# A PEER decoder trunk on one core: the dense output product takes 224 tokens, the last 32 are gathered by index and added on VectorE

## The chip, the core and the metric

The kernel runs on one core of a Trainium2 chip. The metric is the device time of one execution in microseconds. The kernel before took a median of 1882.46 us in three runs (1881.70, 1882.46 and 1882.48).

## The reference, cut to what matters

Two layers, 256 tokens of 1024 columns. Each layer has a trunk (three groups of mixing heads and an output projection) and then a PEER block. In the PEER block every token chooses, for each of 8 heads, 16 of 128 x 128 = 16,384 single-neuron experts, so 128 experts in all, each with a gate:

```python
experts = e1 * N_KEYS + e2                      # (tokens, 128 choices)
gates = softmax(sv)                             # of the 16 best scores per head
hid = gelu(einsum("td,tkd->tk", xi, u_tab[ei])) # one hidden value per token and choice
out = einsum("tk,tkd->td", gates * hid, v_tab[ei])
x = x + out
```

## The kernel before, in words

The kernel doesn't gather. It computes the hidden values of all 16,384 experts for all 256 tokens, multiplies them by a dense matrix of gates that is zero except at the chosen experts, and multiplies the result by the whole table `v`. An expert is a pair (a, j): a lies on the 128 partitions, j runs over 128 steps. All products are made of two float32r parts, hi and lo: hi x hi, lo x hi and hi x lo.

`trunk` makes queries, keys, values, the convolution and the recurrence, and the output projection; `add_rows` (L187 to L209) adds a result of a product to the residual `x` and scales its rows; `norm_tail` (L224) transposes the normed rows into `XH` and `XL` for the next stage. `peer` (L597) has these stages:

- queries and scores, then top-16 searches and decoding on VectorE, which lie beside the first 18 pairs of the hidden product (`J1=36`). `turn` (L737) transposes chosen indices and gates of 128 tokens into `eH`, `eT`, `gT`.
- the hidden product (`hpair`, L811): for a pair j, j+1, 2 x 24 matmuls of 256 columns (L172 to L174) with the blocks of `u` as weights and the normed activations as moving operand. ScalarE applies the GELU into `ab3[:, j, token]`.
- `quad` (L768): for four tokens, 8 matmuls of 128 columns (L798) build the dense gates from one-hot rows that VectorE (L776, L782, L792) and ScalarE (L789) make; the result is multiplied into `ab3` or put where a later `hpair` multiplies it. 64 quads for 256 tokens, spread over the 46 pairs after the first 18.
- the output product (`out_step` L841, `accumulate` L239): for each j the block `v[l, :, j, :]` (128 x 1024, 512 KB, queue SP, L151) is split into hi (ScalarE, L163) and lo (VectorE, L164), the coefficients `ab3[:, j, :]` of 256 tokens into `chl` (ScalarE L846, VectorE L847). The coefficients are the weights of the matmul, `v` is the moving operand: per j two token halves x two column halves x three products, 12 matmuls of 512 columns into four PSUM banks (L250, L251, L252). The last `TAIL=2` steps go bank by bank, so that the first token half is ready before the second.

Three buffers each for `raw`, `hi` and `lo`, two for `chl` (tag `hg`). The order of the instructions on each engine is fixed when the program is built, by a scheduler that follows the order of the source and priorities; `load` and `split` have a high priority, so they run ahead as far as buffers allow.

Of the kernel before, what the change touches and what calls it, by code (L numbers as in the profile page):

```python
# [35 lines left out]
CW = 661  # L36
# [9 lines left out]
def hymba_peer_kernel(  # L46
# [28 lines left out]
    WARM=12,  # L75
):
# [4 lines left out]
    dr_p = ctx.enter_context(tc.tile_pool(name="dr", bufs=1, space=bass.MemoryType.DRAM))  # L81
    xd = [dr_p.tile([P, D], F32, name=f"xd{i}") for i in range(2)]
# [20 lines left out]
    ab3 = ab.rearrange("p (n t) -> p n t", t=T)  # L103

# [36 lines left out]
    # products of zeros: the tensor engine's clock is up when the first rows arrive  # L141
# [11 lines left out]

    def split(r, w=D, after=None):
        hi = spl_p.tile([P, w], F32R, tag="hi", name="hi")
        lo = spl_p.tile([P, w], F32R, tag="lo", name="lo")
        with ExitStack() as es:
            if after:
                for ins in after:
                    es.enter_context(tc.issue_after(ins.ins))  # L160
            else:
                es.enter_context(tc.high_priority(offset=0))
            S.activation(out=hi, in_=r, func=AF.Copy)  # L163
            V.tensor_tensor(out=lo, in0=r, in1=hi.bitcast(F32), op=ALU.subtract)  # L164
# [21 lines left out]
    def add_rows(tt, ps, gb):  # L186
        # the residual, its rows' scales, and its product with the gains  # L187
# [76 lines left out]

    def log1p_exp_neg_abs(dst, z, n, tag):
# [3 lines left out]
        # exp(-|z|) = ((1 - t) / (1 + t)) ** 4 with t = tanh(|z| / 8)  # L269
# [8 lines left out]
        # log1p(e) = 2 atanh(e / (2 + e))  # L278
# [10 lines left out]
    def trunk(l, mx_p, prev, gb):  # L289
# [44 lines left out]
        # values and forget gates, in the layout [token, column]  # L334
# [41 lines left out]
        # log(1 + exp(-|z|)) of the forget gates and of the recurrence's lambda  # L376
# [9 lines left out]
        # cumulative log forget gates as rank-two terms of the logits  # L386
# [29 lines left out]
        # conformer convolution  # L416
# [19 lines left out]
        def layer_norm():  # L436
# [16 lines left out]
            # a Newton step: y (1.5 - 0.5 v y^2)  # L453
# [10 lines left out]
        # gated linear recurrence  # L464
# [30 lines left out]
        def rnn_scan():  # L495
            # -expm1(2 log_a) = tanh(-log_a) (1 + a^2)
# [10 lines left out]
            # sqrt(v) = v y (1.5 - 0.5 v y^2)  # L507
# [11 lines left out]
        # attention  # L519
# [61 lines left out]
        # output projection and residual  # L581
# [13 lines left out]
    def peer(l, oh_p, wq, next_gain):  # L595
# [108 lines left out]
        def decode_index(tt, s):  # L704
            # sum over ranks a of (a == chosen rank) * index[a]
# [31 lines left out]
        def turn(tt):  # L737
            b = bankb()
            for s in range(3):
                TE.transpose(b[:, s * P:(s + 1) * P], ea[:, tt, s, :], ident)  # L740
            sl = slice(tt * P, (tt + 1) * P)
            S.activation(out=eH[:, :, sl], in_=b[:, 0:2 * P].rearrange("p (s t) -> p s t", t=P),
                         func=AF.Copy)
            S.activation(out=eT[:, sl], in_=b[:, P:2 * P], func=AF.Copy)
            # the scaled gate as two float16 parts, each kept as float32
            g = b[:, 2 * P:3 * P]
            gh = sm_p.tile([P, P], F16, name="gh", bufs=1)
# [243 lines left out]
```

## Time and profile before

| | |
|---|---|
| median of the runs shown | 1882.46 us (1881.70 to 1882.48) |
| span of the profiled execution, first to last instruction | 1879.8 us |
| own time of the profiled execution | recorded by its span alone; the runs lie 1.9 to 2.7 us above it |
| TensorE (PE) busy | 1850.7 us, 98% |
| VectorE (DVE), ScalarE (ACT), GpSimd (POOL) busy | 1358.5, 1196.0, 28.1 us |
| TensorE's granted clock | 0.998 of 2.4 GHz over the span |
| moved by DMA | 328.86 MB, mean 175 GB/s |

How to read it: PE is one engine with a fixed order; "busy" counts overlapping matmuls once, and a matmul's own duration is longer than the distance to the next start, because they are pipelined. The rate of a stream is therefore taken from start to start. PEld is the weight load that goes with every matmul. An idle entry names what ended the wait.

### The profile page before, as it was taken

To read this page: it belongs to the slowest core of one execution; us is meant where nothing else is said; L and a number is where in the kernel's file an instruction comes from. 1 tells how busy PE (TensorE), PEld (TensorE's weight loads), DVE (VectorE), ACT (ScalarE), POOL (GpSimd) and SP (SyncE) were. 2 spreads that over 40 slices of the span, in tenths; PEclk is the share of its full clock that TensorE was granted. 3 is DMA by queue.
4 is the path that set the end of the run, shared out by engine and by line. 5 is a ranking of instruction groups with operands and counts; after the bars stand their busy time and mean duration, and the time that the engine had idled before them with its cause. 6 is when DMAs were issued, how large, how long until landed. Compare 5 with 4: busy or idle time off the path is not lost.

```text
span 1879.8 us, 33413 instructions
## 1 busy us (share of the span) xinstructions
PE 1850.7 (98%) x12688; PEld 1672.3 (89%) x12688; DVE 1358.5 (72%) x2902; ACT 1196.0 (64%) x2345; POOL 28.1 (1%) x34
## 2 busy tenths in 40 slices
PE   9999999999999999999999999999999999999998
PEld 8889999999998888888897899999999988888886
DVE  6969987778885555555688699777788755555555
ACT  5954668888874444444469455598888744444444
POOL 0100000000000000000010000000000000000000
PEclk9999999999999999999999999999999999999999
DMA  6264555555555655555543545655555565555554
GB/s 228 91 210 154 168 184 168 160 167 166 163 166 202 211 188 186 188 190 188 184 156 118 174 152 172 193 160 166 168 159 169 167 213 191 186 187 189 190 190 136
DMA packets 90016, 328.86 MB, mean 175 GB/s; under 512 B 9984, under 2 KB 9984, under 8 KB 89600
## 3 DMA queue, kind: packets, MB, share of 16 engines
q1 hardware_dynamic: 88704, 322.54, 52.8%
q10 hardware_dynamic: 1152, 4.19, 0.6%
q8 instruction: 99, 1.62, 0.3%
q14 instruction: 61, 0.50, 0.1%
HBM read 323.55 MB, written 3.15 MB: 174 GB/s over the span
## 4 chain that ended last, share of the span: by engine, by line
PE 89%; DVE 8%; ACT 2%; issue 1%; POOL 0%; DMA 0%; POOLq 0%; SPq 0%; ACTq 0%
PE bank L172 14%; PE bank L174 14%; PE bank L173 14%; PE bankb L251 13%; PE bankb L250 13%; PE bankb L252 13%; PE bankb L798 3%; DVE lo L164 3%; PE bank L651 1%; DVE ab L627 1%; DVE ab L625 1%; DVE ab L626 1%; DVE ab L624 1%; PE bank L231 0%; DVE ab L623 0%
## 5 line engine op out<-in xcount | busy, mean ns | idle before, releaser
L164 DVE TENSOR_TENSOR lo<-raw,hi 128x1024 fp32r<-128x1024 f32 (+1 forms) x600 | 734.1, 1225 | 255.6 <-ACT hi L163 252.1
L163 ACT ACTIVATE hi<-raw 128x1024 fp32r<-128x1024 f32 (+1 forms) x600 | 630.5, 1053 | 262.8 <-PE bank L173 126.3
L172 PE MATMUL bank<-XH,hi 128*128 128x256 f32 x2560 | 732.0, 286 | 0.0
L174 PE MATMUL bank<-XH,lo 128*128 128x256 f32 x2560 | 723.0, 282 | 6.2 <-DVE lo L164 6.2
L173 PE MATMUL bank<-XL,hi 128*128 128x256 f32 x2560 | 719.5, 281 | 0.7 <-DVE XL L236 0.7
L174 PEld LDWEIGHTS bank<-XH,lo 128*128 128x128 f32 x2560 | 483.0, 189 | 8.4 <-DVE lo L164 8.2
L172 PEld LDWEIGHTS bank<-XH,hi 128*128 128x128 f32 x2560 | 484.4, 189 | 1.4 <-issue 0.4
L173 PEld LDWEIGHTS bank<-XL,hi 128*128 128x128 f32 x2560 | 483.5, 189 | 1.1 <-DVE XL L236 1.1
L250 PE MATMUL bankb<-hi,chl 128*128 128x512 f32 x1024 | 406.1, 397 | 1.0 <-ACT chl L846 1.0
L251 PE MATMUL bankb<-lo,chl 128*128 128x512 f32 x1024 | 405.5, 396 | 0.0
L252 PE MATMUL bankb<-hi,chl 128*128 128x512 f32 x1024 | 405.3, 396 | 0.0
L846 ACT ACTIVATE chl<-ab 128x256 fp32r<-128x256 f32 x256 | 106.7, 418 | 361.7 <-PE bankb L252 361.7
L789 ACT ACTIVATE ob<-oe,gT 128x128 f16<-128x128 f16 x768 | 251.9, 407 | 0.9 <-DVE oe L782 0.9
L250 PEld LDWEIGHTS bankb<-hi,chl 128*128 128x128 f32 x1024 | 192.7, 188 | 48.7 <-ACT chl L846 2.4
L252 PEld LDWEIGHTS bankb<-hi,chl 128*128 128x128 f32 x1024 | 192.1, 188 | 47.3 <-DVE chl L847 0.7
L251 PEld LDWEIGHTS bankb<-lo,chl 128*128 128x128 f32 x1024 | 192.6, 188 | 45.4
L847 DVE SCALAR_TENSOR_TENSOR chl<-ab,chl 128x256 fp32r<-128x256 f32 x256 | 108.9, 426 | 157.9 <-ACT chl L846 157.9
L776 DVE TENSOR_TENSOR oa<-iota,eH 128x512 f16<-128x512 f16 x128 | 54.2, 424 | 50.1 <-PE bankb L798 49.3
L798 PE MATMUL bankb<-ob,oa 128*128 128x128 f16 x1024 | 74.0, 222 | 0.0
L792 DVE TENSOR_SCALAR ob<-iota_h,eT,gT 128x128 f16<-128x128 f16 x256 | 70.6, 310 | 0.0
L782 DVE TENSOR_TENSOR oe<-iota,eH 128x512 f16<-128x512 f16 x128 | 53.9, 424 | 20.6 <-ACT ob L789 19.7
L798 PEld LDWEIGHTS <-oa 128*128 128x128 f16 x1024 | 60.2, 115 | 4.0
(198 smaller groups left out, 1171.4 us busy)
## 6 DMA issues: line engine op xcount, KB each, us to landing
raw<-in_u_dram SPq DMA_DIRECT2D x256, 512.0 KB, 3.5
raw<-in_v_dram SPq DMA_DIRECT2D x256, 512.0 KB, 4.2
raw<-in_ws_dram SPq DMA_DIRECT2D x32, 512.0 KB, 3.6
raw<-in_wq_dram SPq DMA_DIRECT2D x32, 512.0 KB, 4.0
raw<-in_wo_dram SPq DMA_DIRECT2D x16, 512.0 KB, 3.8
raw<-in_wv_dram SPq DMA_DIRECT2D x8, 528.0 KB, 3.7
ab<-in_g_dram SPq DMA_DIRECT2D x4, 512.0 KB, 5.8
ab<-in_kt_dram SPq DMA_DIRECT2D x2, 1024.0 KB, 6.7
```

The costliest lines, as they stand in the source:

```text
L163: S.activation(out=hi, in_=r, func=AF.Copy)
L164: V.tensor_tensor(out=lo, in0=r, in1=hi.bitcast(F32), op=ALU.subtract)
L172: TE.matmul(out=ps, lhsT=hi[:, k, :], rhs=XH[:, k, :], start=(k == 0), stop=False)
L173: TE.matmul(out=ps, lhsT=hi[:, k, :], rhs=XL[:, k, :], start=False, stop=False)
L174: TE.matmul(out=ps, lhsT=lo[:, k, :], rhs=XH[:, k, :], start=False, stop=(k == KT - 1))
L250: TE.matmul(out=po, lhsT=mh, rhs=hi[:, d0:d0 + 512], start=(m == 0), stop=False)
L251: TE.matmul(out=po, lhsT=mh, rhs=lo[:, d0:d0 + 512], start=False, stop=False)
L252: TE.matmul(out=po, lhsT=ml, rhs=hi[:, d0:d0 + 512], start=False, stop=(m == n - 1))
L789: S.activation(out=ob[:, s, i, :], in_=oe[:, :, i], func=AF.Copy, scale=gT[:, s, t:t + 1])
L798: TE.matmul(out=b[:, i * P:(i + 1) * P], lhsT=oa[:, :, i], rhs=ob[:, s, i, :], start=(s == 0), stop=(s == 1))
L846: S.activation(out=chl[:, 0, :], in_=c, func=AF.Copy, scale=1.0 / GS)
L847: V.scalar_tensor_tensor(out=chl[:, 1, :], in0=c, scalar=1.0 / GS, in1=chl[:, 0, :].bitcast(F32), op0=ALU.mult, op1=ALU.subtract)
```

## The change

`TG=32` tokens leave the dense path, `TD=224` stay in it.

- The output product is turned (`accumulate_turned`): the blocks of `v` are the weights, 8 blocks of 128 columns, and `chl` is the moving operand. Per j and block one matmul of 448 columns (hi x both parts of `chl`, side by side) and one of 224 (lo x the hi part), 16 matmuls into 8 PSUM banks `ot`. `chl` has two tags now, so four buffers, and is written before the load of its step.
- At the layer's end `finish(d)` adds the two halves of a bank (ScalarE copy, VectorE add) and transposes the block back to rows of tokens (two transposes per block).
- The 32 tokens' hidden values are stored to DRAM, 16 values of j at a time (8 stores per layer on ACT's queue, 128 x 16 x 32 numbers). Then 32 indirect DMAs on POOL's queue read back 128 numbers each (`gathered_hidden`: choice i of every token and head group, onto 128 partitions), 32 more gather 128 rows of `v` each, 512 KB (`gathered_sum`), and 32 operations on VectorE multiply a gathered block by its coefficient and add it up in `aG`. They stand beside the steps j = 28 to 119 of the output product. One matmul of 512 columns per column half with a 0/1 matrix then folds the 128 partitions into 32 token rows.
- 56 quads per layer instead of 64.

```diff
+TG = 32
+TD = T - TG
+NG = P // TG
...
+def accumulate_turned(ot, steps, tail, finish):
+        def block(m, st, d):
+            chl, (hi, lo) = st
+            w = slice(d * P, (d + 1) * P)
+            TE.matmul(out=ot[d][:, 0:2 * TD], lhsT=hi[:, w],
+                      rhs=chl.rearrange("p s t -> p (s t)"), start=(m == 0), stop=False)
+            TE.matmul(out=ot[d][:, 0:TD], lhsT=lo[:, w], rhs=chl[:, 0, :], start=False,
+                      stop=(m == n - 1))
...
+        for d in range(KT):
+            for i, st in enumerate(last):
+                block(n - tail + i, st, d)
+            finish(d)
...
+        def gathered_index():
+            V.scalar_tensor_tensor(out=e, in0=e, scalar=float(P), in1=ea[:, 1, 1, :],
+                                   op0=ALU.mult, op1=ALU.add)
...
+            for g in range(NG):
+                for s in range(2):
+                    TE.matmul(out=b[g * TG:(g + 1) * TG, s * TG:(s + 1) * TG],
+                              lhsT=ident[:, P - TG:P],
+                              rhs=ea[:, 1, 2 * s, g * TG:(g + 1) * TG], start=True, stop=True)
...
+        def gathered_hidden():
+            for i in range(TG):
+                G.indirect_dma_start(out=cG[:, i:i + 1], out_offset=None, in_=hd[l],
+                                     in_offset=bass.IndirectOffsetOnAxis(ap=pos[:, i:i + 1], axis=0))
...
+        def gathered_sum(i):
+            r = carve((3, 4, 6)[i % 3] * D, D)
+            G.indirect_dma_start(out=r, out_offset=None, in_=vr_in,
+                                 in_offset=bass.IndirectOffsetOnAxis(ap=idx[:, i:i + 1], axis=0))
...
+            with tc.issue_after(last_lo[0].ins):
...
+                    V.scalar_tensor_tensor(out=aG, in0=r, scalar=c, in1=aG, op0=ALU.mult,
+                                           op1=ALU.add)
...
+            if j % HSTORE == 0:
+                nc.scalar.dma_start(out=hdv[:, j - HSTORE:j, :], in_=ab3[:, j - HSTORE:j, TD:T])
...
-                chl = oh_p.tile([P, 2, T], F32R, tag="hg", name="chl")
-                w = split(load(v_in[l, :, j, :]))
-                c = ab3[:, j, :]
+                chl = oh_p.tile([P, 2, TD], F32R, tag=("hg", "ob")[j // 2 % 2], name="chl")
+                c = ab3[:, j, 0:TD]
...
-            while tq[0] < T // 4 and tq[0] < (jp + 1) * (T // 4) / (rest - QLEAD):
+            while tq[0] < TD // 4 and tq[0] < (jp + 1) * (TD // 4) / (rest - QLEAD):
...
-        pr = [bankb() for _ in range(4)]
+        gathered_hidden()
+        ot = [bankb() for _ in range(4)] + [bank() for _ in range(4)]
...
+        for i in range(TG):
+            j = GHEAD + i * (P - GTAIL - GHEAD) // TG
+            steps[j] = with_sum(i, steps[j])
...
+        def finish(d):
+            tb = carve(9 * D + (d % 2) * TD, TD)
+            S.activation(out=tb, in_=ot[d][:, TD:2 * TD], func=AF.Copy)
+            V.tensor_tensor(out=oT[:, d, :], in0=ot[d][:, 0:TD], in1=tb, op=ALU.add)
+            dh, q = divmod(d, 4)
+            if q == 0:
+                y.append([bankb(), bankb()] if dh == 0 else [bankb(), bankb()])
+                TE.matmul(out=y[dh][1][P - TG:P, :], lhsT=cst[:, CSEL:CSEL + TG],
+                          rhs=aG[:, dh * 512:(dh + 1) * 512], start=True, stop=True)
+            TE.transpose(y[dh][0][:, q * P:(q + 1) * P], oT[:, d, 0:P], ident)
+            TE.transpose(y[dh][1][0:P - TG, q * P:(q + 1) * P], oT[:, d, P:TD], ident)
-        accumulate(pr, steps, TAIL)
-        return pr, gains[0]
+        accumulate_turned(ot, steps, TAIL, finish)
+        return [y[0][0], y[1][0], y[0][1], y[1][1]], gains[0]
```

**Where instructions move.** POOL before, in the first layer's PEER block (L665 clears the candidates, L183 is the power in `row_scale`):

```order
L665 MEMSET ab 128x512 x2
L183 TENSOR_TENSOR ss<-ss,cst 128x1 x2
L411 TENSOR_SCALAR ab<-ab,cst 16x256 x8
L183 TENSOR_TENSOR ss<-ss,cst 128x1 x2
L665 MEMSET ab 128x512 x2
```

and now:

```order
L748 MEMSET ab 128x512 x2
L682 DMA cG<-hd_60,pos 128x1 x32
L692 DMA ab<-in_v_dram,idx 128x1024 x32
L196 TENSOR_TENSOR ss<-ss,cst 128x1 x2
L446 TENSOR_SCALAR ab<-ab,cst 16x256 x8
```

Between the memsets and the power of the next norm there are now 64 indirect DMAs in one queue, all reads of hidden values ahead of the first rows of `v`. At most eight are under way at once: each waits for the one eight places before it, and a gather of rows waits besides for the sum three before it, whose buffer it takes.

VectorE in the stretch of the output product that has the sums (L177 is the split of L164, L934 the coefficients of L847, L701 the sum):

```order
L177 TENSOR_TENSOR lo<-raw,hi 128x1024 [waits DMAHW7_49,PE_49,Activation_49]
L701 SCALAR_TENSOR_TENSOR ab<-ab,cG 128x1024 [waits DMASW4_49,DVE_49]
L934 SCALAR_TENSOR_TENSOR chl<-ab,chl 128x224 [waits Activation_49]
L177 TENSOR_TENSOR lo<-raw,hi 128x1024 [waits DMAHW0_49,PE_49,Activation_49]
L934 SCALAR_TENSOR_TENSOR chl<-ab,chl 128x224 [waits Activation_49]
```

A sum stands behind the split of its step and ahead of the next step's coefficients, and waits for its gather (DMASW).

TensorE at the end of the first layer's output product, before (L252 the last product, L231 the next layer's norm):

```order
L250 MATMUL bankb<-hi,chl 128x512
L251 MATMUL bankb<-lo,chl 128x512
L252 MATMUL bankb<-hi,chl 128x512
L231 MATMUL bank<-dg,ab 128x128 [waits DVE_49]
L231 MATMUL bank<-dg,ab 128x128 x3
```

and now, from the third of the eight blocks on (L985 folds the gathered rows, L987 and L988 are transposes):

```order
L285 MATMUL bankb<-chl,hi 128x448
L985 MATMUL bankb<-ab,cst 32x512 [waits DVE_49]
L988 MATMUL bankb<-cst,ab 96x128 [waits DMASW6_49]
L287 MATMUL bankb<-chl,lo 128x224
L285 MATMUL bankb<-chl,hi 128x448
L987 MATMUL bankb<-cst,ab 128x128 [waits DVE_49]
L987 MATMUL bankb<-cst,ab 128x128
L988 MATMUL bankb<-cst,ab 96x128
L287 MATMUL bankb<-chl,lo 128x224
```

The fold and the transposes stand among the last blocks' products and wait for VectorE's additions; the last block's own transposes stand behind its last product, ahead of the next norm.

## Rows read from the trace of the kernel before

**Rows 1.** The page's first part: busy time of each engine, share of the span, instructions.

```profile
span 1879.8 us, 33413 instructions
PE 1850.7 (98%) x12688; PEld 1672.3 (89%) x12688; DVE 1358.5 (72%) x2902; ACT 1196.0 (64%) x2345; POOL 28.1 (1%) x34
```

**Rows 2.** The page's fourth part: the chain that ended last, by engine.

```profile
PE 89%; DVE 8%; ACT 2%; issue 1%; POOL 0%; DMA 0%; POOLq 0%; SPq 0%; ACTq 0%
```

**Rows 3.** Windows: a short stretch with much loading, the hidden product with quads, the output product. Columns: stretch, its length, busy us and instructions of PE, PEld, DVE, ACT, POOL, granted clock, DMA share, GB/s.

```profile
265.00:270.00 5.00, 5.00 (x45) 5.00 (x43) 3.83 (x4) 2.20 (x3) 0.00 (x0) 1.00 0.73 247
300.00:400.00 100.00, 100.00 (x936) 99.27 (x935) 75.33 (x163) 87.01 (x223) 0.00 (x0) 1.00 0.51 164
800.00:900.00 100.00, 100.00 (x430) 80.51 (x430) 59.19 (x73) 48.92 (x72) 0.00 (x0) 1.00 0.57 188
```

**Rows 4.** Timeline of the output product: start, duration, engine, line. The first and the last of the rows are the same place of two successive steps, 12 matmuls apart; between them the step's work on ACT and DVE.

```profile
760.16 0.40 PE L250 MATMUL bankb<-hi,chl 128*128 128x512 f32 x1
...
761.76 0.42 ACT L846 ACTIVATE chl<-ab 128x256 fp32r<-128x256 f32 x1 [1.43 <-PE bankb L252]
...
762.09 1.04 ACT L163 ACTIVATE hi<-raw 128x1024 fp32r<-128x1024 f32 x1
...
762.22 0.43 DVE L847 SCALAR_TENSOR_TENSOR chl<-ab,chl 128x256 fp32r<-128x256 f32 x1 [0.62 <-ACT chl L846]
...
762.96 0.40 PE L250 MATMUL bankb<-hi,chl 128*128 128x512 f32 x1
...
763.16 1.23 DVE L164 TENSOR_TENSOR lo<-raw,hi 128x1024 fp32r<-128x1024 f32 x1 [0.52 <-ACT hi L163]
```

**Rows 5.** Timeline of PE in the hidden product: 46 successive matmuls of 256 columns (first and last), then a quad and the two matmuls behind it.

```profile
398.05 0.28 PE L174 MATMUL bank<-XH,lo 128*128 128x256 f32 x1
...
403.38 0.28 PE L174 MATMUL bank<-XH,lo 128*128 128x256 f32 x1
403.50 0.64 PE L798 MATMUL bankb<-ob,oa 128*128 128x128 f16 x8
403.95 0.36 PE L172 MATMUL bank<-XH,hi 128*128 128x256 f32 x1
404.15 0.28 PE L173 MATMUL bank<-XL,hi 128*128 128x256 f32 x1
```

**Rows 6.** Three float32 transposes of 128 columns in a row on PE (timeline), and the mean of one (groups by line).

```profile
226.64 0.49 PE L740 MATMUL bankb<-cst,ab 128*128 128x128 f32 x3
```

```profile
L740 PE MATMUL bankb<-cst,ab 128*128 128x128 f32 x12 | 2.0, 272 | 0.0
```

**Rows 7.** Groups by line and form: busy us, mean ns of one | idle before, releaser.

```profile
L164 DVE TENSOR_TENSOR lo<-raw,hi 128x1024 fp32r<-128x1024 f32 x592 | 724.1, 1225 | 254.8 <-ACT hi L163 251.3 <-PE bank L174 2.6 <-issue 0.3
L163 ACT ACTIVATE hi<-raw 128x1024 fp32r<-128x1024 f32 x592 | 621.9, 1052 | 261.3 <-PE bank L173 126.3 <-issue 79.5 <-DMA raw<-in_u_dram 21.8
L645 ACT ACTIVATE ab<-bank 128x256 f32<-128x256 f32 x32 | 11.7, 364 | 0.0
L320 DVE TENSOR_TENSOR ML<-bankb,MH 128x256 fp32r<-128x256 f32 x8 | 3.4, 425 | 4.0 <-ACT MH L319 4.0
L183 POOL TENSOR_TENSOR ss<-ss,cst 128x1 f32<-128x1 f32 x10 | 8.7, 870 | 1739.1 <-DVE ss L181 1732.1 <-DMA cst<-in_cst_dram 7.0
```

**Rows 8.** Loads of `v` between 640 and 900 us: the issue on SP's queue (ns, min/median/max), and the time to landing.

```profile
L151 SPq DMA_DIRECT2D raw<-in_v_dram x93: 327/328/328, 641.2 to 898.8; - x93
DMA to landing us min/median/max: 3.3/3.5/5.2
```

**Rows 9.** DMA issues on ACT's queue and SP's of the page's sixth part: KB each, median us from issue to landing.

```profile
ab<-xd ACTq DMA_DIRECT2D x4, 512.0 KB, 5.1
out_dram<-ab SPq DMA_DIRECT2D x4, 256.0 KB, 2.1
```

**Rows 10.** Timeline at the end of the first layer: PE's last product, the first token half's scale, the next norm.

```profile
940.57 0.40 PE L252 MATMUL bankb<-hi,chl 128*128 128x512 f32 x1
940.58 0.63 ACT L195 ACTIVATE ab<-ab 128x512 f32<-128x512 f32 x1 [0.54 <-DVE ab L193]
940.76 0.86 POOL L183 TENSOR_TENSOR ss<-ss,cst 128x1 f32<-128x1 f32 x1 [800.52 <-DVE ss L181]
941.12 0.19 ACT L195 ACTIVATION_READ_ACCUMULATOR ab<-ab 128x1 f32 x1
941.65 0.29 DVE L214 TENSOR_SCALAR dg<-cst,ss 128x128 f32<-128x128 f32 x1 [0.44 <-POOL ss L183]
941.85 0.68 DVE L193 TENSOR_TENSOR ab<-ab,bankb 128x512 f32<-128x512 f32 x1
941.99 0.38 PE L231 MATMUL bank<-dg,ab 128*128 128x128 f32 x1 [1.03 <-DVE dg L214]
```

**Rows 11.** Timeline at the end of the program: PE's last product, the addition that follows it, the last scale.

```profile
1872.06 0.39 PE L252 MATMUL bankb<-hi,chl 128*128 128x512 f32 x1
...
1872.48 0.69 DVE L193 TENSOR_TENSOR ab<-ab,bankb 128x512 f32<-128x512 f32 x1
...
1875.57 0.72 ACT L889 ACTIVATE ab<-ab,ss 128x512 f32<-128x512 f32 x1 [1.29 <-POOL ss L183]
```

More of the change, by code (lines that the diff above doesn't have):

```diff
@@ L75, in hymba_peer_kernel @@
     WARM=12,
+    HSTORE=16,
+    GHEAD=28,
+    GTAIL=6,
 ):
@@ L81, in hymba_peer_kernel @@
     dr_p = ctx.enter_context(tc.tile_pool(name="dr", bufs=1, space=bass.MemoryType.DRAM))
+    hd = [dr_p.tile([P * P * TG, 1], F32, name=f"hd{i}") for i in range(DEPTH)]
     xd = [dr_p.tile([P, D], F32, name=f"xd{i}") for i in range(2)]
@@ L263, in accumulate @@
                     one_half(n - tail + i, st, tt, (dh,))
+    def accumulate_turned(ot, steps, tail, finish):
+        n = len(steps)
+        def block(m, st, d):
[5 more added lines that the diff above has]
+                      stop=(m == n - 1))
+        for m in range(n - tail):
+            st = steps[m]()
+            for d in range(KT):
+                block(m, st, d)
+        last = [steps[m]() for m in range(n - tail, n)]
+        for d in range(KT):
+            for i, st in enumerate(last):
+                block(n - tail + i, st, d)
+            finish(d)
     def log1p_exp_neg_abs(dst, z, n, tag):
@@ new lines, in peer @@
+        gG = oh_p.tile([P, TG], F32, name="gG", bufs=1)
+        cG = oh_p.tile([P, TG], F32, name="cG", bufs=1)
+        aG = carve(5 * D, D)
+        hdv = hd[l].rearrange("(e j t) o -> e j (t o)", e=P, t=TG)
+        def gathered_index():
+            e = ea[:, 1, 0, :]
+            V.scalar_tensor_tensor(out=e, in0=e, scalar=float(P), in1=ea[:, 1, 1, :],
+                                   op0=ALU.mult, op1=ALU.add)
+            b = bankb()
+            for g in range(NG):
[3 more added lines that the diff above has]
+                              rhs=ea[:, 1, 2 * s, g * TG:(g + 1) * TG], start=True, stop=True)
+            V.tensor_scalar(out=idx, in0=b[:, 0:TG], scalar1=float(l * NX), scalar2=None,
+                            op0=ALU.add)
+            V.tensor_scalar(out=pos, in0=b[:, 0:TG], scalar1=float(TG),
+                            scalar2=cst[:, CTOK:CTOK + 1], op0=ALU.mult, op1=ALU.add)
+            V.tensor_copy(out=gG, in_=b[:, TG:2 * TG])
@@ new lines, in gathered_sum @@
+        def gathered_sum(i):
+            r = carve((3, 4, 6)[i % 3] * D, D)
+            G.indirect_dma_start(out=r, out_offset=None, in_=vr_in,
+                                 in_offset=bass.IndirectOffsetOnAxis(ap=idx[:, i:i + 1], axis=0))
+            if i % (TG // 2) == 0:
+                gathered_gate(i // (TG // 2))
+            c = cG[:, i:i + 1]
+            with tc.issue_after(last_lo[0].ins):
+                if i == 0:
+                    V.tensor_scalar(out=aG, in0=r, scalar1=c, scalar2=None, op0=ALU.mult)
+                else:
+                    V.scalar_tensor_tensor(out=aG, in0=r, scalar=c, in1=aG, op0=ALU.mult,
+                                           op1=ALU.add)
@@ L849, in f @@
                                        op0=ALU.mult, op1=ALU.subtract)
-                return (chl[:, 0, :], chl[:, 1, :]), w
+                w = split(load(v_in[l, :, j, :]))
+                return chl, w
             return f
@@ L860, in peer, with with_sum, g, with_reload @@
             hpair()
-        pr = [bankb() for _ in range(4)]
+        gathered_hidden()
+        ot = [bankb() for _ in range(4)] + [bank() for _ in range(4)]
         steps = [lambda b=b: b for b in begun] + [out_step(j) for j in range(len(begun), P)]
         gains = []
-        def with_reload():
-            for tt in range(2):
-                nc.scalar.dma_start(out=x[tt], in_=xd[tt])
-            gains.append(load_gain(next_gain, 0))
-            return out_step(P // 2)()
-        steps[P // 2] = with_reload
-        accumulate(pr, steps, TAIL)
-        return pr, gains[0]
+        def with_sum(i, f):
+            def g():
+                st = f()
+                gathered_sum(i)
+                return st
+            return g
+        for i in range(TG):
+            j = GHEAD + i * (P - GTAIL - GHEAD) // TG
+            steps[j] = with_sum(i, steps[j])
+        def with_reload(f):
+            def g():
+                for tt in range(2):
+                    nc.scalar.dma_start(out=x[tt], in_=xd[tt])
+                gains.append(load_gain(next_gain, 0))
+                return f()
+            return g
+        steps[P // 2] = with_reload(steps[P // 2])
+        oT = carve(3 * D, KT, TD)
+        y = []
+        def finish(d):
[11 more added lines that the diff above has]
+        return [y[0][0], y[1][0], y[0][1], y[1][1]], gains[0]
     prev = None
```

41 lines of the change are left out of this document (29 added, 12 removed).

## The prediction

> **What bounds the kernel now.** I read the page's busy times first, then the chain that ended last, then windows of the two long stages, then timelines of PE. PE is busy 98% of the span [rows 1] and carries 89% of the chain [rows 2]; in the hidden product and in the output product it is busy 100 of 100 us, at full granted clock, while VectorE has 25% and 41% to spare and the DMA engines work half the time [rows 3]. So the time is the sum of PE's streams, and a change counts by the columns that it takes from PE, as long as nothing else becomes late. The reader should not take a matmul's duration (0.40 us) for its price: the next starts much earlier. One step of the output product takes 762.96 - 760.16 = 2.80 us for 12 matmuls of 512 columns, 0.2333 us each [rows 4]. In the hidden product 45 distances of 256 columns take 403.38 - 398.05 = 5.33 us, 0.1184 us each [rows 5]. A line through both gives 0.449 ns per column and 3.4 ns per matmul.
>
> **What the change takes from PE.** *The output product.* A step now has 8 pairs of 448 and 224 columns, 5376 in place of 6144. By the line a pair costs 0.2046 + 0.1040 = 0.3086 us and a step 2.469 us. But a weight load goes with each matmul, and the rows have no float32r matmul under 256 columns. The nearest rows bound the shorter one: three float32 transposes of 128 columns stand (0.49 - 0.27) / 2 = 0.11 us apart [rows 6], so a load can follow a load after 0.11 us at most, and 256 columns after 0.1184 us. The price of 224 columns lies between 0.1040 and 0.1184 us; I take 0.107, near the transposes, since they bound the load more closely. Pair 0.3116, step 2.493 us; 256 steps save 256 x (2.800 - 2.493) = 78.6 us. Ends: 84.7 us at 0.1040, 55.3 us at 0.1184.
>
> The Trainium skill (TensorE: Matmul & The Clock Gate, Back-to-back issue gap) gives columns / 2.4 + 2.5 ns at the full clock. By that rule a pair would cost 285 ns, a step 2.28 us, and the saving would be 133 us. The trace disagrees: the rule's 215.8 ns for 512 columns is 233 here [rows 4], so the rows' line stands.
>
> *Quads.* Eight matmuls take 403.95 - 403.50 = 0.45 us, and the distance behind them is 0.20 in place of 0.118 [rows 5]: 0.53 us a quad, 16 fewer, 8.5 us. Sixteen short matmuls of the index are added, at most 0.11 us each [rows 6]; I take 1 us for them. Net 7.5 us.
>
> **What it adds on PE's path: the end of each layer.** PE gets two folds of 512 float32 columns, four times 0.11 us each [rows 6], and 16 transposes at 0.11: 2.6 us. They wait. Before a block's transposes ScalarE must copy and VectorE add: the reader starts 0.2 us after the next matmul could (1872.48 against 1872.06 + 0.23 [rows 11]); 0.36 us for the copy and 0.43 for the addition [rows 7], and two hops of 0.1: 1.2 us. I laid the order of the rows out with these prices. The first fold uses the bank of the second block and stands one matmul behind it: PE waits 1.0 us. The third block's transposes wait 0.55, the seventh's 0.4, and the last block's, with nothing left to do, 1.2. Together 3.1 us, with the 2.6 of work 5.7 us. Then both token halves become complete at the same moment, where before the first was ahead. The path from the last transpose to the next norm has an addition of 0.68, square and read 0.82, 0.21 for the sum, POOL's 0.86, 0.29 for the scaled identity and some 0.7 of hops: 3.5 us, against 941.99 - 940.80 = 1.2 us before [rows 10]. PE's second wait of 0.4 us there goes. So 7.7 us in the middle. At the program's end the last row ends as before, 0.7 us later for the second addition in front of it: 6.4 us. Sum 14 us; bounds 8 (waits hidden, as in a better overlap) and 22 (every wait doubled).
>
> **What is added beside PE.** *VectorE.* A step costs 1.225 + 0.38 us now, and 32 sums per layer, 1.23 us each if they go like the split, which reads two inputs of 1024 too [rows 7], come every 2.9 steps: 2.03 of 2.49 us. This hides; `chl` has a buffer pair more, and the split runs up to three steps ahead, so a sum of 1.2 us fits in. *ScalarE* has 1.43 us a step, and eight stores per layer whose issue I cost at the 0.33 us of an issue on SP's queue [rows 8]; 128 numbers of runs of 128 B may take longer, but the three buffers of `raw` and `hi` cover some 2 us. *DMA.* In the steps with gathers 512 KB x (1 + 32/91) come in 2.49 us, 284 GB/s. 188 GB/s took a share of 0.57 [rows 3], so this takes 0.86; 247 GB/s went at 0.73 beside a full PE. A load of `v` lands after 3.5 us in the median [rows 8]; a third buffer comes free every 7.48 us, and conversion takes 1.05 + 1.23 of that [rows 7], so 5 us are allowed. I cost collisions at 4 us, between 0 and 38 (below). *POOL.* 64 gathers per layer. The first sum stands on VectorE ahead of the coefficients of step 29, so all 32 readings and one gather must be done in 28 steps less a lead of two and the landing of the last store: some 60 us, 1.8 us a gather. No row has one. From below: an issue on another queue, 0.33 us [rows 8]; from above: one after the other at the 5.1 us of a read-back from DRAM [rows 9]. With eight in flight 5.1 us makes 0.64 each, and POOL's smallest operation takes 0.87 [rows 7]: I take about 1 us, which is hidden, and later gathers have three sums' time, 21 us.
>
> **Sum.** -78.6 - 7.5 + 14 + 4 = -68 us. From the profiled span of 1879.8 us this gives 1811.7 us; the median run lies 2.7 us above that span, so I forecast 1814 us. With the kindest terms: -84.7 - 8.5 + 8 = -85, 1797 us.
>
> **Rivals.**
> 1. *The weight load bounds the short matmul* at 0.1184 us. For it: in the hidden product PEld is busy 99% [rows 3]. Against it: the transposes at 0.11 [rows 6]. It gives back 23 us: 1837 us.
> 2. *The loads of `v` become late* in the 182 steps with gathers. If each took the longest landing seen, 5.2 us [rows 8], and a share of a sum, 0.42, with conversion 2.28 and hops 0.2, three buffers would yield a step per 2.70 us, 38 us more than 2.49: 1848 us. For it: three buffers and a DMA share of 0.86. Against it: a landing of 3.5 us would allow 2.13.
> 3. *Slower than before: the gathers on POOL are dear.* VectorE takes its work in order, so a first sum that waits holds every later split, and PE starves. Per layer 33c - 60 us are lost at a price of c per gather. The gain of 68 us is gone at c = 2.85 us; at 5.1 us [rows 9] the loss is 108 us a layer and the time 2030 us. For it: no row shows a gather, and 64 stand in one queue. Against it: eight may be under way.
> 4. *Gathers held up by VectorE*: POOL's work on each has to wait out a split twice, 0.87 + 2 x 1.23 = 3.3 us [rows 7]. 49 us are lost a layer: 1912 us. For it: VectorE is busy some 80% of each step here. Against it: POOL's power took its usual 0.86 us beside an addition and a scaling on VectorE [rows 10]. The Trainium skill (SBUF — State Buffer, SBUF: two separate sides) says that GpSimd is locked out of a port pair that it shares with VectorE while VectorE runs an instruction that takes both ports, and can't write the descriptors of its DMAs then. No run here shows it yet.
>
> That the change doesn't do what it says is excluded by the order: 16 matmuls of 448 and 224 columns stand where 12 of 512 stood.
>
> **How the numbers follow.** The forecast has a chance of 0.62 (1797 to 1832 us), rival 1 0.12, rival 2 0.14, rival 3 0.05, rival 4 0.05, and 0.02 goes to a loss that eats the gain just up. From 1797 to 1850 us the range holds the forecast and the first two rivals, less their edges, some 0.82. A measurement of this kernel can tell about 0.2%, 4 us, from no change. Faster by more: forecast, rivals 1 and 2, 0.88; within: 0.02; slower: rivals 3 and 4, 0.10.
>
> **What would show it.** In the changed profile, steps of the output product 2.47 to 2.51 us apart (2.58: rival 1); the same distance in its first 28 steps as beside the gathers (longer there alone: rival 2); VectorE's sums with idle time of under a microsecond, none of it on the first (tens of microseconds there: rivals 3 and 4); at a layer's end 5 to 6 us between the last block's products and the last transposes, PE idle in four pieces. The forecast is wrong if the hidden product becomes longer than before, which the stores could do, or if PE waits for VectorE in every third step.

## The result: 0.6% slower, where 3.6% faster was forecast

| | before | after |
|---|---|---|
| median | 1882.36 us (1881.70 to 1882.48, 4 runs) | 1893.75 us (1891.81 to 1894.20, 4 runs) |
| span of the profiled execution | 1879.8 us | 1892.4 us |
| granted TensorE clock over the span | 0.998 | 0.978 |
| forecast | | 1814 us (1797 to 1850) |

The ratio is 1.0059, with a 95% interval of 1.0045 to 1.0074: slower by more than the 0.2% that a measurement can tell. Against the forecast of -68 us, some 80 us are missing.

**The busy time** answers to [rows 1], and the chain's summary to [rows 2]. First the page's busy row and its slices of TensorE's work and clock, then the chain by engine:

```profile
PE 1794.2 (95%) x13656; PEld 1715.9 (91%) x13656; DVE 1377.7 (73%) x2914; ACT 1164.0 (62%) x2255; POOL 163.2 (9%) x162
...
PE   9999999999996799999999999999999958999997
...
PEclk9999999999997899999999999999999988999999
...
PE 80%; DVE 8%; DMA 4%; POOL 3%; ACT 2%; issue 2%; POOLq 0%; SPq 0%; ACTq 0%; DVEq 0%
```

TensorE is busy 56 us less. But its slices have two holes, one per layer, where before there was none, and at the same places its clock falls. The chain leaves TensorE there: its share falls from 89% to 80%, and DMA and POOL, which held nothing, hold 7%. VectorE's 8% was there before.

**Who waits for what** (the waits of all engines: who, at which line, for whom; us in total, times, longest):

```profile
DVE cG L688 <- DMA cG<-hd,pos: 76.3, 4, 20.9
...
PE bankb L287 <- DVE lo L177: 61.3, 7, 17.2
```

Line 688 is not a sum. It is the product of the coefficients with their gates, two small operations per layer. These lines of the change issue it (they fell under the dots of the diff above):

```python
def gathered_gate(h):
    sl = slice(h * TG // 2, (h + 1) * TG // 2)
    V.tensor_tensor(out=cG[:, sl], in0=cG[:, sl], in1=gG[:, sl], op=ALU.mult)   # L688
# in gathered_sum(i), between the gather of rows and the sum:
    if i % (TG // 2) == 0:
        gathered_gate(i // (TG // 2))
    c = cG[:, i:i + 1]
    with tc.issue_after(last_lo[0].ins):     # holds the sum, not the gate
```

**VectorE and TensorE at the first hole** (timelines: start, us, engine, line, operation, idle before and its releaser):

```profile
586.28 1.23 DVE L177 TENSOR_TENSOR lo<-raw,hi 128x1024 fp32r<-128x1024 f32 x1 [0.76 <-ACT hi L176]
587.42 0.39 DVE L934 SCALAR_TENSOR_TENSOR chl<-ab,chl 128x224 fp32r<-128x224 f32 x1
608.74 0.18 DVE L688 TENSOR_TENSOR cG<-cG,gG 128x16 f32<-128x16 f32 x1 [20.93 <-DMA cG<-hd,pos]
608.87 1.22 DVE L177 TENSOR_TENSOR lo<-raw,hi 128x1024 fp32r<-128x1024 f32 x1
...
629.13 0.18 DVE L688 TENSOR_TENSOR cG<-cG,gG 128x16 f32<-128x16 f32 x1 [17.30 <-DMA cG<-hd,pos]
```

```profile
592.61 0.38 PE L285 MATMUL bankb<-chl,hi 128*128 128x448 f32 x1
610.15 0.56 PE L287 MATMUL bankb<-chl,lo 128*128 128x224 f32 x1 [17.17 <-DVE lo L177]
...
630.62 0.56 PE L287 MATMUL bankb<-chl,lo 128*128 128x224 f32 x1 [12.38 <-DVE lo L177]
```

Both gates stand far ahead of the sums that use them: behind the coefficients of step 5 and of step 7 (counted from 0), though the first sum comes at step 28. VectorE stands there until 16, then all 32 of POOL's readings (128 numbers each) have landed, and every split is queued behind. Each hole ends with a matmul that takes 0.56 us, at a clock that has fallen meanwhile (windows below).

**POOL's queue** in the same stretch (first and last reading, first gather of rows), and **the clock** (windows: stretch, length, busy us and instructions of PE, PEld, DVE, ACT, POOL, granted clock, DMA share, GB/s). The last window answers to [rows 3]:

```profile
586.62 1.94 POOL L682 DMA_INDIRECT cG<-hd,pos  x1 [446.28 <-DMA ab<-xd]
...
626.70 0.94 POOL L682 DMA_INDIRECT cG<-hd,pos  x1 [0.30 <-issue]
648.96 0.94 POOL L692 DMA_INDIRECT ab<-in_v_dram,idx  x1 [21.32 <-DVE chl L934]
```

```profile
590.00:608.00 18.00, 2.98 (x19) 2.57 (x17) 0.00 (x0) 1.34 (x2) 13.61 (x15) 0.66 0.04 8
608.00:612.00 4.00, 1.85 (x6) 1.76 (x7) 3.10 (x5) 0.00 (x0) 3.08 (x4) 0.50 0.22 60
...
700.00:800.00 100.00, 99.96 (x638) 95.03 (x637) 77.21 (x96) 54.48 (x83) 15.30 (x13) 1.00 0.81 279
```

A reading costs 0.94 us and 0.30 to the next: 1.25 us, 32 of them some 40 us. Meanwhile TensorE stood, and the granted clock of 608 to 612 us is 0.50, its lower level of 1.2 GHz. In the window from 700 us on TensorE is fully busy again, at full clock, and the DMA share is 0.81 (0.86 forecast).

**The step of the output product**, answering to [rows 4], and **the first sum**:

```profile
655.88 0.37 PE L285 MATMUL bankb<-chl,hi 128*128 128x448 f32 x1
...
658.38 0.37 PE L285 MATMUL bankb<-chl,hi 128*128 128x448 f32 x1
```

```profile
683.28 0.75 DVE L699 TENSOR_SCALAR ab<-ab,cG 128x1024 f32<-128x1024 f32 x1
```

The same place of successive steps is 2.507 us apart in the median (2.80 before, 2.493 forecast), and the first sum (L699) waits for nothing. The loss is in four steps per layer: 22.00, 3.26, 17.21 and 3.25 us in the first, 21.89, 2.67, 17.76 and 2.71 in the second. Less 4 x 2.507 each, that is 35.7 + 35.0 = 70.7 us.

### The profile page after: what moved, and what is told of

Read it like the earlier page. It is cut to its first block, busy times and chain, and to the rows that moved or that the text cites. A ratio compares the mean times of both kernels' runs of the same rounds, so it can differ in the third digit from the quotient of the medians.

```text
span 1892.4 us, 35826 instructions
## 1 busy us (share of the span) xinstructions
PE 1794.2 (95%) x13656; PEld 1715.9 (91%) x13656; DVE 1377.7 (73%) x2914; ACT 1164.0 (62%) x2255; POOL 163.2 (9%) x162
## 4 chain that ended last, share of the span: by engine, by line
PE 80%; DVE 8%; DMA 4%; POOL 3%; ACT 2%; issue 2%; POOLq 0%; SPq 0%; ACTq 0%; DVEq 0%
PE bank L185 14%; PE bank L187 14%; PE bank L186 14%; PE bank L285 9%; PE bankb L285 9%; PE bankb L287 5%; PE bank L287 5%; DVE lo L177 3%; POOL cG L682 3%; DMA raw<-in_v_dram 3%; PE bankb L883 3%; ACT hi L176 1%; PE bank L734 1%; PE bankb L265 1%; DVE ab L710 1%
## 5 line engine op out<-in xcount | busy, mean ns | idle before, releaser
L177 DVE TENSOR_TENSOR lo<-raw,hi 128x1024 fp32r<-128x1024 f32 (+1 forms) x600 | 733.4, 1224 | 303.2 <-ACT hi L176 297.8
L285 PE MATMUL bankb<-chl,hi 128*128 128x448 f32 x1024 | 342.1, 378 | 2.3 <-DVE chl L934 2.3
L285 PE MATMUL bank<-chl,hi 128*128 128x448 f32 x1024 | 341.1, 377 | 0.0
L287 PE MATMUL bankb<-chl,lo 128*128 128x224 f32 x1024 | 275.3, 269 | 61.4 <-DVE lo L177 61.3
L287 PE MATMUL bank<-chl,lo 128*128 128x224 f32 x1024 | 273.9, 267 | 0.0
L287 PEld LDWEIGHTS bankb<-chl,lo 128*128 128x128 f32 x1024 | 198.2, 194 | 64.0 <-DVE lo L177 64.0
L285 PEld LDWEIGHTS bankb<-chl,hi 128*128 128x128 f32 x1024 | 194.6, 190 | 18.4 <-DVE chl L934 2.9
L285 PEld LDWEIGHTS bank<-chl,hi 128*128 128x128 f32 x1024 | 194.0, 189 | 17.1 <-issue 1.7
L287 PEld LDWEIGHTS bank<-chl,lo 128*128 128x128 f32 x1024 | 197.2, 193 | 0.0
L934 DVE SCALAR_TENSOR_TENSOR chl<-ab,chl 128x224 fp32r<-128x224 f32 x256 | 98.2, 384 | 0.9 <-ACT chl L933 0.9
L933 ACT ACTIVATE chl<-ab 128x224 fp32r<-128x224 f32 x256 | 95.3, 373 | 2.6 <-DVE ab L907 2.6
```

The source lines that it names most:

```text
L177: last_lo[0] = V.tensor_tensor(out=lo, in0=r, in1=hi.bitcast(F32), op=ALU.subtract)
L285: TE.matmul(out=ot[d][:, 0:2 * TD], lhsT=hi[:, w], rhs=chl.rearrange("p s t -> p (s t)"), start=(m == 0), stop=False)
L287: TE.matmul(out=ot[d][:, 0:TD], lhsT=lo[:, w], rhs=chl[:, 0, :], start=False, stop=(m == n - 1))
L933: S.activation(out=chl[:, 0, :], in_=c, func=AF.Copy, scale=1.0 / GS)
L934: V.scalar_tensor_tensor(out=chl[:, 1, :], in0=c, scalar=1.0 / GS, in1=chl[:, 0, :].bitcast(F32), op0=ALU.mult, op1=ALU.subtract)
```

## The experiments

**1. The gates behind the splits of their own steps.**

```diff
             if i % (TG // 2) == 0:
-                gathered_gate(i // (TG // 2))
+                with tc.issue_after(last_lo[0].ins): gathered_gate(i // (TG // 2))
```

> The changed kernel (1893.75 us) with its two gate products per layer queued on VectorE behind the split of their own step (steps 28 and 75), in place of step 6 and 8. Theory A, VectorE stands at the gates until POOL has issued the readings (steps of 22.0, 3.26, 17.2 and 3.25 us in place of 2.507: 35.7 us in layer 1, 35.0 in layer 2): 1893.75 - 70.7 = 1823 us, no step of the first ten over 4 us. Theory B, the 32 readings themselves hold VectorE or PE back (their descriptors or their traffic), wherever the gates stand: 1885 to 1894 us. Theory C, the readings are too slow even for step 28 and the wait moves there: over 1840 us, a step of over 10 us near step 28; the readings took 1.25 us each from 586.6 us on, so they should be in at 629 us, some 15 us ahead of it.

Measured: 1823.43 us (1822.99 to 1831.86), ratio to before 0.9703 (0.9679 to 0.9727). VectorE's timeline at the gate and the first sum, and the readings (ns min/median/max):

```profile
648.58 1.22 DVE L177 TENSOR_TENSOR lo<-raw,hi 128x1024 fp32r<-128x1024 f32 x1
649.72 0.17 DVE L688 TENSOR_TENSOR cG<-cG,gG 128x16 f32<-128x16 f32 x1
...
650.11 0.75 DVE L699 TENSOR_SCALAR ab<-ab,cG 128x1024 f32<-128x1024 f32 x1
```

```profile
L682 POOL DMA_INDIRECT cG<-hd,pos x64: 940/1134/1989, 586.6 to 1540.2; - x64
```

No idle time at the gate. The same 64 readings are made, on average more slowly than in the changed kernel (1.23 for 0.98 us), and 70 us go. Theories B and C fall. Below this kernel is called the mended one.

**2. The gates on POOL.**

```diff
-            V.tensor_tensor(out=cG[:, sl], in0=cG[:, sl], in1=gG[:, sl], op=ALU.mult)
+            G.tensor_tensor(out=cG[:, sl], in0=cG[:, sl], in1=gG[:, sl], op=ALU.mult)
```

> The changed kernel with the gate products on POOL, in its queue between the readings and the first row gather. Theory A: the wait stands on POOL, where nothing is behind it but row gathers that are due 20 us later, and the time is 1823 us as with the gates behind the splits. Theory B (the readings hold the other engines back): 1885 to 1894 us.

Measured: 1825.55 us (1825.27 to 1825.82). The wait is the same wait, in a queue where nobody is behind it. What counts is not that an instruction waits, but on which engine.

**3. Half the readings.**

```diff
-            for i in range(TG):
+            G.memset(cG, 0.0)
+            for i in (*range(0, TG // 4), *range(TG // 2, 3 * TG // 4)):
```

> The gates stay where they are in the changed kernel, but only the first 8 tokens of each half of 16 are read back; the other 16 coefficients are zero, so their rows add nothing. Theory A: each gate waits for 8 issues of 1.25 us less, 10 us; the two lost 19.5 and 15.8 us a layer and now 9.5 and 5.8: 1893.75 - 40 = 1854 us. Rival: the wait is a fixed latency (stores landing, or a semaphore that comes with the last of a group), not 1.25 us per reading: 1880 to 1894 us.

Measured: 1866.93 us (1866.51 to 1867.36), 27 us back where 40 were expected. VectorE's timeline:

```profile
598.72 0.17 DVE L689 TENSOR_TENSOR cG<-cG,gG 128x16 f32<-128x16 f32 x1 [10.99 <-DMA cG<-hd,pos]
608.82 0.17 DVE L689 TENSOR_TENSOR cG<-cG,gG 128x16 f32<-128x16 f32 x1 [9.93 <-DMA cG<-hd,pos]
```

The price per reading is confirmed: the second gate is done at 608.82 in place of 629.13 us, 20.3 us for 16 readings, 1.27 each. The sum was wrong in another place: the two gates stand back to back now. In the changed kernel two splits ran between them, and TensorE worked two steps there. So the stall halves, and TensorE's loss only falls from 35.4 to about 20 us a layer (in the first, steps of 22.17 and 3.16 us). The steps give 30 us back; 3.7 us of it are lost again behind the last product, at the program's end of this profile, and why is open.

**4. The turned product alone.** The edit takes out `gathered_hidden()`, the 32 `with_sum` and the stores, and clears `aG`.

> The changed kernel without anything for the last 32 tokens: no stores of their activations, no readings, no row gathers, no sums; their output rows get nothing from this layer. Theory A: the turned product of 224 tokens runs at 2.507 us a step throughout; 1893.75 - 70.7 for the gates and some 6 us more for the late steps beside the gathers (0.3 to 1.3 us each, some 5 in all) and the first step: 1817 us. If the turned product itself were what takes the time back, it would stay above 1870 us.

Measured: 1821.27 us (1820.90 to 1821.65). All that the 32 tokens add beside the stream, 64 indirect DMAs, 16.8 MB of rows and 32 sums a layer, costs 2 to 3 us when no one waits for it at the wrong place. The late steps were put too high: the first step of each layer (3.84 us) is there without the tokens, too.

**5. The sums earlier.** Experiment 1 with `GHEAD=8` and `GHEAD=16` in place of 28. The buffers of gathered rows lie over coefficients of the steps 12 to 27, which are still needed then: some of those steps use overwritten numbers, and their coefficients also wait for the sums, so only the first wait of each kernel is read.

> The kernel with the gates behind their splits (1823.4 us), the sums spread from step 8 on in place of 28. Theory A: VectorE would come to the first gate some 3 us ahead of step 8 of PE, at 597 us; the 16 readings that it needs were 1.49 us apart beside a working VectorE (32 of them from 586.6 to 634.3 us), so they are in at 586.6 + 24 + 2.3 = 613 us with VectorE working and at 609 us with it standing. A wait of 12 to 14 us, of which PE loses about 12 a layer: 1847 us (1840 to 1855). The second gate stands at step 65 and doesn't wait. Theory D, only what stands in the first steps of the stage costs (a pipeline that isn't filled yet), and a wait at step 8 is covered by the loads that are ahead: under 1828 us.

> The same with the sums from step 16 on. Theory A: VectorE comes to the first gate at 578.6 + 1.4 + 16 x 2.507 - 3 = 617 us, 4 us behind the landing of reading 16: no wait, 1823 us (1820 to 1827). If each gate needed all 32 readings (in at 637 us) it would wait 20 us and PE lose some 18 a layer: 1859 us.

Measured: 1874.54 us (1872.57 to 1878.26) and 1869.31 us (1868.32 to 1870.31). VectorE's timelines, from step 8, then from step 16:

```profile
596.32 1.22 DVE L177 TENSOR_TENSOR lo<-raw,hi 128x1024 fp32r<-128x1024 f32 x1 [0.26 <-ACT hi L176]
609.98 0.17 DVE L688 TENSOR_TENSOR cG<-cG,gG 128x16 f32<-128x16 f32 x1 [12.44 <-DMA cG<-hd,pos]
```

```profile
617.57 0.17 DVE L688 TENSOR_TENSOR cG<-cG,gG 128x16 f32<-128x16 f32 x1
...
635.89 0.75 DVE L699 TENSOR_SCALAR ab<-ab,cG 128x1024 f32<-128x1024 f32 x1 [17.85 <-DMA ab<-in_v_dram,idx]
```

The gate at step 8 waits 12.44 us, as worked out; the gate at step 16 doesn't wait, as worked out. The totals miss. From step 16 the reason stands in the last row: the first sum waits for its rows, whose gather is queued on POOL behind all 32 readings. My expectation had followed the gate alone. The forecast's condition for the first sum (all readings and one gather) is the right one for a sum, and step 28 leaves it some 14 us.

**6. Three rows only, the mended kernel again, and a tail of three.** The first leaves out 29 of 32 row gathers (`if i < 3:` ahead of the gather); the last sets `TAIL=3`. The tail of three was run on two chips.

> The kernel with the gates behind their splits, with the last three steps in place of two taken block by block, so that each block's products last 0.94 in place of 0.63 us while the block before it is copied, added and turned. The layer ends of 18.9 and 20.0 us hold 1.2 us of waiting before the first fold, 0.24 between blocks, 0.88 before the last transposes and 3.1 before the norm. If the forecast's short waits between blocks were what made the ends longer than forecast, they go: 1819 us or less. If the serial path behind the last block makes them, at most a microsecond a layer goes: 1821 to 1824 us, not told from 1823.4.

> The kernel with the gates behind their splits once more, beside the two below on one chip. Its four runs gave 1823.0 to 1831.9 us and the kernel with a tail of three 1828.3 to 1838.0 on another chip, while before stays within 1.5 us. Theory T (traffic): the loads of the output product, which share the DMA engines with row gathers, come late now and then, by an amount that changes from run to run and chip to chip: again 1822 to 1835 us with a spread of several us. If the spread is chance of one run: 1822 to 1825 us throughout.

> The same kernel with only the first 3 row gathers of each layer; the other 29 sums are made over the rows that lie in the three buffers, so the last 32 tokens' rows are not the reference's. VectorE's sums stay where they were, the traffic of 29 x 512 KB a layer goes. Theory T: the late steps beside the sums go with the gathers, the time is that of the turned product alone plus what the first gathers cost, 1820 to 1823 us, and the runs lie within 1 to 2 us. Theory V (the sums on VectorE make the splits late): as the kernel above, within 2 us of it, with the same spread.

> The tail of three again, beside the tail of two on one chip. Its layer ends in the trace were 1.2 and 0.8 us shorter than with two; what was longer lay in late steps at the begin of the sums (3.70, 3.92 and 4.97 us). Theory T, these are chance of run and chip: within 3 us of the kernel with the tail of two. If the longer tail causes them: again some 10 us above it.

Measured: tail of three 1833.12 us (1828.25 to 1837.97), then beside each other on one chip: the mended kernel 1824.15 us (1822.28 to 1826.38; ratio 0.9694, 0.9681 to 0.9707), three rows 1821.75 us (1821.17 to 1822.42), tail of three 1830.19 us (1827.65 to 1833.69). Windows of the mended kernel, then of three rows:

```profile
700.00:800.00 100.00, 99.89 (x638) 95.02 (x637) 76.61 (x97) 53.23 (x80) 14.46 (x14) 1.00 0.85 279
```

```profile
700.00:800.00 100.00, 100.00 (x640) 95.44 (x639) 76.65 (x98) 53.33 (x81) 0.00 (x0) 1.00 0.70 210
```

The gathers of rows raise the DMA share from 0.70 to 0.85 and cost about 2 us; with them the runs lie 4 us apart, without them 1.3. In the profiles the late steps from step 28 on add up to 2.7 us with them and to 0.6 without. VectorE does the same work in both, so the runs favour theory T over V, though the intervals of the two ratios touch. The mended kernel's second set of runs doesn't tell chance from traffic.

The tail of three met none of the times expected for it. That its ends were 1.2 and 0.8 us shorter, as the last expectation has it, came of counting from step 126, which lies inside a tail of three. From the first product of step 125 to the next stage (second run on the one chip):

```profile
893.78 0.37 PE L285 MATMUL bankb<-chl,hi 128*128 128x448 f32 x1
...
894.99 0.68 PE L285 MATMUL bankb<-chl,hi 128*128 128x448 f32 x2 [0.42 <-ACT hi L176]
...
917.22 0.57 PE L383 MATMUL bankb<-hi,XH 128*128 128x264 f32 x1
```

That is 23.4 us; in the mended kernel beside it, 895.82 to 917.27, it is 21.45. In the second layer, to the program's end, it is 24.95 for 22.48. Both profiles of the tail of three give the same, so its ends are 2.0 and 2.5 us longer, 4.5 of the 6 us between the medians. The first block now waits for the splits of three steps, and the short waits between blocks don't go: there are four of 0.24 to 0.25 us in the first layer, where the tail of two has one.

**7. The short matmul.** Experiment 1 with the low part's matmul cut to 192 and to 128 columns: `ot[d][:, 0:192]`, `chl[:, 0, 0:192]`, and the same with 128.

> The kernel with the gates behind their splits (1823.4 and 1824.2 us), the matmuls of the low parts cut from 224 to 192 columns: the low parts of 32 tokens are left out. It prices the term that the forecast took at 0.107 us for 224 columns; the step of 2.507 us gives 2.507 / 8 - 0.2046 = 0.1088. If columns set it (0.449 ns each), a pair gives 14.4 ns back, a step 0.115 us: 2.392 us, 256 of them 29 us, 1795 us. If the weight load already sets it at 224 columns, the step stays at 2.507 us and the time at 1824 us. Anything between is a floor between 0.094 and 0.109 us.

> The same with 128 columns: the low parts of 96 tokens are left out. If columns alone set it, 8 x 96 x 0.449 ns = 0.345 us a step: 2.162 us, 1736 us, or more where loads of 2.162 us with row gathers ask more than the DMA engines give. If a weight load sets a floor, the step is the same as with 192 columns, and its excess over 8 x 0.2046 us is eight times that floor.

The totals, 1857.03 us (1854.72 to 1859.34) and 1844.36 us (1832.51 to 1856.21), are no measure of the matmul: their loads stood still for a time (last section). The steps are. TensorE's timelines, the same place of two steps, with 192 and with 128 columns:

```profile
597.30 0.39 PE L285 MATMUL bankb<-chl,hi 128*128 128x448 f32 x1
597.53 0.25 PE L287 MATMUL bankb<-chl,lo 128*128 128x192 f32 x1
...
599.81 0.39 PE L285 MATMUL bankb<-chl,hi 128*128 128x448 f32 x1
```

```profile
597.36 0.42 PE L285 MATMUL bankb<-chl,hi 128*128 128x448 f32 x1
597.62 0.22 PE L287 MATMUL bankb<-chl,lo 128*128 128x128 f32 x1
...
599.89 0.42 PE L285 MATMUL bankb<-chl,hi 128*128 128x448 f32 x1
```

2.51 us with 192 columns and 2.50 to 2.53 with 128, as with 224. Columns don't set the short matmul at any of these sizes. By the 0.2046 us that the prediction's line gives the long one, an estimate, what stays is 2.507 / 8 - 0.2046 = 0.109 us a pair. That it is the weight load that takes them is argued: no run changed the loads.

The Trainium skill (TensorE: Matmul & The Clock Gate, LDWEIGHTS) gives a weight load its columns / 1.2 in ns: an estimate of 107 ns for 128 columns. The floor of 109 ns worked out here agrees.

## Why the forecast was wrong, point by point

**The step that failed** is the one on POOL: "The first sum stands on VectorE ahead of the coefficients of step 29, so all 32 readings and one gather must be done in 28 steps". The sum stands there. But that sum isn't the first instruction on VectorE that waits for the readings; the gate is, and nothing ties the gate to its sum. It stood in VectorE's order, to be read before any run (L934 writes a step's coefficients, L177 splits a block of `v`):

```
L177 TENSOR_TENSOR lo<-raw,hi 128x1024 [waits DMAHW1_49,PE_49,Activation_49]
L934 SCALAR_TENSOR_TENSOR chl<-ab,chl 128x224 [waits DVE_49,Activation_49]
L688 TENSOR_TENSOR cG<-cG,gG 128x16 [waits DMASW4_49,DMASW5_49,DMASW3_49,DMASW6_49,DMASW2_49,DMASW7_49,DMASW1_49,DMASW0_49]
L177 TENSOR_TENSOR lo<-raw,hi 128x1024 [waits DMAHW3_49,PE_49,Activation_49]
```

I looked at the stretch with the sums alone. So the readings were given some 60 us of cover, and had about 1 us: VectorE came to the gate at 587.8 us, 1.2 us after POOL's first reading. The sign that the prediction set for a late reading, idle time on the first sum, couldn't show it: by then the gates had waited, and the first sum has none.

**Price and mechanism came apart.** Rivals 3 and 4 are refuted by their prices: a reading takes 1.25 to 1.6 us from start to start, near the forecast's "about 1 us" (a guess between 0.33 and 5.1), and not 2.85 or more. Rival 4's mechanism does exist, at a smaller price (last section). But the mechanism of rival 3, that VectorE takes its work in order and a waiting instruction holds every later split, is what happened, from another instruction. With the price known, the loss could have been worked out: from 587.8 to 629.1 us VectorE stands, 41.3 us; less two steps of 2.5 us between the gates, 36 us a layer, beside the 35.4 measured.

**The other terms**, from the spans of before and of experiment 1 (1879.84 and 1821.62 us), where the wait is gone:

| term | forecast | measured | how |
|---|---|---|---|
| output product's steps | -78.6 | -76.6 | 126 steps of 2.507 for 353.56 us a layer, and 0.6 for the last two |
| quads, index | -7.5 | -6.7 | trunk and hidden product 564.71 for 567.69, and 565.48 for 569.19 us |
| ends of layer and program | +14 | +18.1 | 18.87 for 8.72, 19.98 for 13.21 us from step 126 on, and 0.6 each |
| first and late steps | +4 | +7.0 | 319.64 and 319.09 us for 126 x 2.507 |
| sum | -68 | -58.2 | |
| wait at the gates | 0 | +70.8 | span of after less that of experiment 1 |

The first row holds the first step of before, too (3.46 us, 0.66 over the others).

*Steps.* That something other than columns bounds the short matmul, as in rival 1, holds (experiment 7), at another price: not the 0.1184 us of 256 columns, but 0.109, next to the transposes' 0.11 [rows 6]. 0.002 us a pair, 3.6 us in all, by which the 2.507 lies above 2.493. By the rule of 285 ns a pair that the prediction set beside its line, the step would be 2.28 us; a pair takes 313 ns.

*Ends.* Too small by 4 us, inside the bounds of 8 and 22. Two terms were mis-sized, the folds and the work behind the longest wait. In the changed kernel, the first fold and the matmul behind it, then the last product, the last transposes, the norm's transposes and the next stage's first product, answering to [rows 10], and the window of the norm:

```profile
936.45 1.05 PE L985 MATMUL bankb<-ab,cst 128*32 128x512 f32 x2 [1.21 <-DVE ab L981]
937.42 0.32 PE L988 MATMUL bankb<-cst,ab 128*96 128x128 f32 x1
...
944.38 0.35 PE L287 MATMUL bank<-chl,lo 128*128 128x224 f32 x1
945.60 0.33 PE L987 MATMUL bankb<-cst,ab 128*128 128x128 f32 x1 [0.87 <-DVE ab L981]
945.77 0.27 PE L988 MATMUL bankb<-cst,ab 128*96 128x128 f32 x1
949.15 3.75 PE L244 MATMUL bank<-dg,ab 128*128 128x128 f32 x16 [3.11 <-DVE ss L194]
952.56 0.57 PE L383 MATMUL bankb<-hi,XH 128*128 128x264 f32 x1
```

```profile
949.00:952.50 3.50, 3.35 (x16) 3.38 (x17) 1.65 (x5) 0.60 (x1) 0.86 (x1) 0.50 0.00 0
```

A fold is two matmuls of 512 columns, 0.49 us each, 0.98 us in place of the 0.44 forecast: 2.1 us more for the four folds of both layers. The path to the norm, forecast at 3.5 us, takes 949.15 - 945.77 = 3.4. What I left out comes behind that wait: the granted clock is 0.50, the lower level, and the 16 transposes up to the next product take 3.4 us. In the kernel before TensorE waited 1.03 us at that place [rows 10], the clock stayed at 1.00, and the same 16 took 1.9 us (941.99 to 943.89 us):

```profile
942.00:944.00 2.00, 2.00 (x17) 1.96 (x18) 1.75 (x4) 1.21 (x3) 0.26 (x1) 1.00 0.00 0
```

That is 1.5 us, in the first layer alone. A longer wait was priced at its length; it also took the clock from the work behind it.

*First and late steps.* The gathers cost 2 to 3 us (experiments 4 and 6). 1.4 us a layer come from the first two steps (3.84 and 2.61 us): the last pair's GELU and product stand ahead of step 1's coefficients, and TensorE waits 1.14 us. I had not looked there. Rival 2 is refuted: the steps beside the gathers are 2.507 us apart in the median like the others, at a DMA share of 0.81 to 0.85.

## What to carry to other kernels

When a change lets an engine wait for something slow, find every instruction on that engine that depends on it, the small ones above all, and read where each stands in the order; an anchor on one of them doesn't move the others. On an engine that feeds the critical one, put the waiting instruction behind the work that must not wait, or on an engine with nothing behind it: here one line was worth 70 us and turned 0.6% slower into 3% faster. A small operation's duration (0.18 us) says nothing of what it costs.

## What the runs showed of the hardware

- A short matmul behind a long one cost about 0.109 us (worked out above) whatever its columns: 224, 192 and 128 gave the same step within 0.02 us. So here more tokens off the dense path would save on the long matmul alone.
- A reading by index of 128 numbers takes POOL 0.94 us, and longer when it starts while VectorE is at work. VectorE's and POOL's timelines in experiment 1, where the DMA share was 0.74:

```profile
588.70 1.23 DVE L177 TENSOR_TENSOR lo<-raw,hi 128x1024 fp32r<-128x1024 f32 x1 [0.98 <-ACT hi L176]
588.78 1.97 POOL L682 DMA_INDIRECT cG<-hd,pos  x1 [0.31 <-issue]
591.06 0.94 POOL L682 DMA_INDIRECT cG<-hd,pos  x1 [0.30 <-issue]
591.51 1.23 DVE L177 TENSOR_TENSOR lo<-raw,hi 128x1024 fp32r<-128x1024 f32 x1 [1.28 <-ACT hi L176]
```

  The first reading starts in a split and ends 0.82 us behind the split's end; the second starts with VectorE idle and isn't longer for the split that begins meanwhile. So it goes throughout: 36 of the 64 readings start while a split or the coefficients run on for at least 0.12 us, and 35 of these end 0.81 to 0.82 us behind that instruction; of the other 28, 27 take 0.94 to 0.95 us. It goes by VectorE's instruction and not by the DMA traffic, which both kinds had. The Trainium skill (SBUF — State Buffer, SBUF: two separate sides) speaks of a lock between the two engines, which the one that starts first keeps for its whole instruction; these rows agree with it.
- In the kernel with 192 columns the loads of `v` stopped for some 20 us while POOL read back in layer 2. Windows there (columns as above):

```profile
1512.00:1524.00 12.00, 8.99 (x49) 7.57 (x48) 3.11 (x5) 1.42 (x3) 9.26 (x10) 0.91 0.61 210
1524.00:1530.00 6.00, 3.43 (x10) 2.17 (x9) 1.53 (x2) 1.34 (x2) 4.78 (x5) 0.50 0.02 0
1530.00:1540.00 10.00, 4.75 (x10) 3.13 (x11) 0.00 (x0) 0.00 (x0) 7.06 (x8) 0.50 0.17 53
```

  From 1524 to 1530 us the DMA engines have nothing to do (share 0.02) though loads had been issued by 1519 us, and TensorE starves. Both kernels of experiment 7 show late steps there, of up to 13.80 us with 192 columns and up to 7.88 with 128; the seven profiles of experiments 1, 2, 4 and 6 show no step of over 5 us there. Its cause is open.
